# Differential attention's q and k kept in SBUF, and its scores taken as three 32-row products per map

## The chip, the cores and the metric

The kernel is one program on one core of a Trainium2 chip. The metric is the device time of one execution in microseconds (us); lower is better. The cores' engines are named as the profile names them: PE (TensorE matmul), PEld (its weight loads), DVE (VectorE), ACT (ScalarE), POOL (GpSimd), SP (SyncE, which here only issues DMAs).

## What is computed

Two layers of a block on 1024 tokens of width 1024. Each layer normalises x, projects it by `w_in` (1024 x 2472), and feeds three mixers whose outputs are joined and projected by `w_out`; then a squared-ReLU MLP of width 4096 follows. The three mixers are differential attention, latent attention (MLA) and a state space part with a short convolution. Only the first matters here, cut from the reference:

```python
DA_HEADS = 4; DA_QK = 32; DA_V = 64
q = q.reshape(b, s, DA_HEADS, 2, DA_QK)      # two maps per head
k = k.reshape(b, s, DA_HEADS, 2, DA_QK)
s1 = einsum('bqhd,bkhd->bhqk', q1b, k1) * DA_QK ** -0.5
s2 = einsum('bqhd,bkhd->bhqk', q2b, k2) * DA_QK ** -0.5
p = masked_softmax(s1, mask) - lam * masked_softmax(s2, mask)
o = einsum('bhqk,bkhe->bqhe', p, v)          # mask: chunks of 64 keys up to the query's own chunk
```

## The kernel before

Every large product is made from operands split in two float32r parts, `hi` and `lo`. The helper `mm3` (lines 189 to 193) issues hi·hi, hi·lo and lo·hi one after another into the same PSUM bank; these are lines L191, L192 and L193 of the profile. Split operands live in one SBUF tile, `split`, that is cut into numbered slots (`slot`, line 142); float32 scratch lives in `arena_f`. PSUM is two double banks (`bank_s`, `bank2`, line 139) and four single ones (`bank_t`, `bank_a`, `bank_b`).

One layer's mixer (line 1175) is written as Python generators that are woven together by shares: the in-projection `in_proj` (line 569), differential attention `attention` over four `da_head` generators (line 763), the state space part, MLA, and the loads of `w_out`. The program order that results is then reordered on each engine by the tile framework's scheduler, so that the order on PE is not that of the source; within an engine the instructions run in the order that the scheduler left.

`in_proj` walks through `w_in` by chunks of columns, with a chunk's weights loaded, and split by ACT (line 545) and by DVE or POOL (line 546), one chunk ahead. The first chunk holds q and k of the heads 0 and 1 ("pair 0", 128 feature rows each: two heads of two maps of 32 rows), then come v, MLA's low-rank columns (128x424 products), the six convolution chunks, with q and k of pair 1 between them, and z. Beside it, in layer 0 alone, a background stream (`mod_chunk`, line 408) loads 512 KB pieces of `w_ada` (line 415, on SP), multiplies them on POOL (L434), sums them on DVE (L436) and ends with tiny products on PE (L441, L443).

q and k of a pair leave PSUM feature-major in `qk` (line 595): ACT writes the hi part (L600), DVE the lo part (L601), into a ring of two half slots. Then POOL issues two DMAs per piece (L605) that write it to the DRAM tensor `d_qk` twice, so that the four blocks of 32 rows hold hi, hi, lo, lo for q and hi, lo, hi, lo for k. `da_head` (line 763) reads them back, for each map one DMA on POOL (L770) of 1024 KB, into a ring of three slots with all 128 rows filled. Thereby one product with 128 rows is the sum of all four of hi·hi, hi·lo, lo·hi and lo·lo:

```python
nc.tensor.matmul(S[:, c0:c1], Q[mp][:, tok], K[mp][:, c0:c1], start=True, stop=c1 < n)          # L786
nc.tensor.matmul(S[:, n - 64:n], self.chunk[:, 0:P], self.chunk[:, P:192], start=False, stop=True)  # L787
```

For each head, each of eight query tiles t and each of two maps this is one product per 512 keys out of n = 128 (t+1), and a mask product (L787) of 64 columns with a rank-one operand `chunk`. Then DVE takes the maximum (L723), ACT the exponential (L724), DVE joins the two maps (L794 to L797), PE transposes the probabilities (L749), ACT copies them (L752), PE multiplies them with v (L736), transposes the result (L759) and DVE scales it (L761). In the state space part, L1052 transposes rows that were read back from the DRAM tensor `d_xbc` (L1041), L1043 reads another part of it, L1063 uses that, and L1101 and L814 write results to `d_cc`. The first two heads run beside the in-projection's middle chunks, the last two beside z, the state space part and the start of MLA.

Of the kernel before, what the change touches and what calls it, by code (L numbers as in the profile page):

```python
# [11 lines left out]
F32R = mybir.dt.float32r  # L12
# [5 lines left out]
P = 128  # L18
T = 1024
NT = T // P  # L20
D = 1024
KD = D // P
# [22 lines left out]
class Arena:  # L45
    """Words of one tile, given out where they have been free for longest."""
# [12 lines left out]
    def _find(self, m, top):  # L59
        """Large pieces start at whole blocks; small ones keep to blocks already broken where they can."""  # L60
# [47 lines left out]
class Net:  # L108
    def __init__(self, ctx, tc, ins):
# [9 lines left out]
        # split operands: nine slots of 2048 words, then two blocks of a whole [KD, T]  # L119
# [11 lines left out]
    @contextmanager  # L131
    def phase(self, **banks):
        """The four single PSUM banks, by use."""
        with self.tc.tile_pool(name="psum", bufs=1, space=bass.MemoryType.PSUM, reuse_waits="tile") as self.psum:
            self.banks = banks
            yield
        self.psum = None
# [4 lines left out]
    def slot(self, i, *shape, off=0):  # L142
        """Words of the split operands from slot i on."""
# [8 lines left out]
    def ring(self, name, slots, *shape):  # L152
        """The next of the slots in turn."""
# [7 lines left out]
    def rsqrt(self, ssq, n, scale, eps):  # L161
        """1/sqrt(ssq*scale+eps) for [P, n] in plain arithmetic: a seed from the exponent, then Newton steps."""
# [15 lines left out]
    def rstd(self, ssq, y=None):  # L178
        """1/sqrt(ssq/D + eps) for [P, 1]: the table's root, then a Newton step."""
# [16 lines left out]
    def mlp(self, l, hT, y, bg, late, finish):  # L196
        """y = relu(h @ w_up)^2 @ w_down in groups of hidden tiles; finish(t) is called as each tile of y is complete."""
# [39 lines left out]
        for g, size in enumerate(GROUPS):  # L237
# [4 lines left out]
            if g == 0:  # L242
                # by halves of the tokens: the last tiles of h come later
# [37 lines left out]
    def setup(self):  # L281
# [5 lines left out]
        # rank-one products that mask the keys of a block's second chunk for the queries of its first  # L287
        m = F.get(192)
        nc.gpsimd.memset(m, 0.0)
        nc.gpsimd.memset(m[0:1, 0:64], -1.0e30)  # L290
        nc.gpsimd.memset(m[0:1, 128:192], 1.0)
# [7 lines left out]
        # silu(c), feature 8p+k at [p, k]  # L299
# [15 lines left out]
        self.d_qk = [dt(f"d_qk{l}", [4, 2 * P, 2, T], F32R) for l in range(DEPTH)]  # L315
# [5 lines left out]
    def rope_tables(self):  # L321
# [29 lines left out]
        # [cos | cos] and [-sin | sin]  # L351
# [56 lines left out]
    def mod_chunk(self, l, sec, q, W, lag=None):  # L408
        """W columns of section sec as a row of the DRAM table, in steps: the loads, the products, the sums.
        Without a lag the products run on the vector engine; with one Pool has them, and the sums follow so many steps  # L410
        later."""
# [43 lines left out]
    def mod_stream(self, todo, per, lag=None):  # L455
        """todo: arguments of mod_chunk; chunks run staggered, one started every so many steps."""
# [28 lines left out]
    def norm(self, x, a, b, xn, eng=None):  # L485
        """xn = (x*rstd)*a + b."""
# [25 lines left out]
    def finish(self, y, src, g, dst, t, x, u, junk):  # L512
        """x += rms(y)*g for one tile of tokens; y [P, D] in PSUM or SBUF; u and x hold [P, D], u may be y."""
# [10 lines left out]
    def stage_w(self, w, cols, step=None):  # L524
        """w[:, cols] for the column ranges given, as loads still to be split."""
# [12 lines left out]
    def load_w(self, stage, slot, eng=None):  # L538
        """hi/lo of staged columns as [P, 2, k, n] from a slot on."""
# [29 lines left out]
    def in_proj(self, l, hT, st, bg, late):  # L569
        """h @ w_in by chunks of columns, its weights one chunk ahead; yields after each PSUM bank or two.  # L570
        q, k of a pair of heads go to DRAM feature-major, v stays, the low-rank part goes to DRAM token-major,
        the convolved part feature-major; z is used at once by the state space part."""
# [5 lines left out]
        # the columns and the slot of each chunk  # L578
        chunks = [(pair(0), 2), (run(C_V), 0), (run(C_CQ, 212), 6), ([(C_CQ + 212, C_Z), (C_DT, C_DT + 8)], 2)]
        chunks += [(run(C_XBC, P), 5), (run(C_XBC + P), 6), (run(C_XBC + 3 * P), 2), (pair(1), 6), (run(C_XBC + 5 * P, P), 2)]  # L580
# [832 lines left out]
```

## Time and profile before

| what | value |
|---|---|
| runs, median (lowest to highest) | 2979.09 us (2963.41 to 2982.9), 3 runs |
| profiled execution | its time is known by its span alone, 2975.8 us: 3.3 us under the median of the runs |
| mean granted TensorE clock | 0.947 |
| PE, DVE, ACT, POOL busy | 90%, 52%, 32%, 21% of the span |
| DMA traffic | 273.19 MB, of it 33.58 MB on POOL's queue |
| `d_qk<-split` (L605) | 32 DMAs of 512 KB |
| `split<-d_qk` (L770) | 16 DMAs of 1024 KB |

In rows of the timeline the columns are: start in us, duration in us, engine, line, operation, output<-input, shapes, count, and in brackets how long the engine stood idle before it and what ended that. A matmul's duration is a latency; since matmuls are pipelined, what one costs is read from the distance between starts. In rows of the windows each engine's busy time is followed by its count of instructions, then come the granted clock, the share of DMA engines' time that was busy, and GB/s. In rows of the waits: total us, times, longest.

### The profile page before, as it was taken

What the parts mean: (1) busy time and instruction counts of PE and PEld (TensorE: products, weight loads), DVE (VectorE), ACT (ScalarE), POOL (GpSimd) and SP (SyncE); (2) the same over time, 40 slices, a digit from 0 to 9 for tenths busy, and PEclk for the clock granted to TensorE, in tenths of its full rate; (3) what the DMA queues carried; (4) which work ended last, traced back from release to release, by engine and by line L of the source; (5) the groups of instructions that cost most, each with busy time, mean ns of one, the idle gap of its engine ahead of it and who ended that gap; (6) DMA issues with size and microseconds to landing.
All of it is one profiled execution on the core that took longest, in us unless ns stands there. A gap on an engine that the chain in (4) does not pass through costs nothing. (4 is left out here: it accounts for less than half of the span.)

```text
span 2975.8 us, 33230 instructions
## 1 busy us (share of the span) xinstructions
PE 2683.2 (90%) x12402; PEld 2113.0 (71%) x12402; DVE 1554.6 (52%) x2861; ACT 941.5 (32%) x1827; POOL 623.3 (21%) x558
## 2 busy tenths in 40 slices
PE   5678779899899999999978895897998999999998
PEld 4556556676687877887757674665767888888887
DVE  7557457543835566666491563565446133433334
ACT  5233334544531112112242442344444221221222
POOL 1422224310311111111151122342003001111113
PEclk9889989899999999999989997898999999999999
DMA  6962632321423233233344245222123111111112
GB/s 215 197 113 85 154 74 77 113 70 43 164 78 100 79 99 104 74 107 91 99 139 108 64 125 104 66 86 92 56 99 113 43 50 50 57 43 44 57 43 99
DMA packets 275846, 273.19 MB, mean 92 GB/s; under 512 B 29730, under 2 KB 233700, under 8 KB 273636
## 3 DMA queue, kind: packets, MB, share of 16 engines
q1 hardware_dynamic: 258532, 237.47, 26.9%
q0 software_dynamic: 17152, 33.58, 5.3%
q8 instruction: 98, 1.61, 0.2%
q14 instruction: 64, 0.52, 0.1%
HBM read 221.34 MB, written 49.65 MB: 91 GB/s over the span
## 5 line engine op out<-in xcount | busy, mean ns | idle before, releaser
L191 PE MATMUL bank_b<-split 128*128 128x512 f32 (+2 forms) x1952 | 770.7, 395 | 30.0 <-ACT split L545 16.3
L192 PE MATMUL bank_b<-split 128*128 128x512 f32 (+2 forms) x1952 | 758.0, 388 | 9.5 <-DVE split L510 8.2
L193 PE MATMUL bank_b<-split 128*128 128x512 f32 (+2 forms) x1952 | 756.1, 388 | 1.2 <-DVE split L210 0.6
L191 PE MATMUL bank_s<-split 128*128 128x512 f32 (+2 forms) x1152 | 453.4, 396 | 8.8 <-ACT arena_f L724 3.9
L192 PE MATMUL bank_s<-split 128*128 128x512 f32 (+2 forms) x1152 | 449.9, 391 | 5.4 <-DVE split L1305 4.7
L191 PEld LDWEIGHTS bank_b<-split 128*128 128x128 f32 x1952 | 375.9, 193 | 110.7 <-ACT split L545 17.1
L193 PE MATMUL bank_s<-split 128*128 128x512 f32 (+2 forms) x1152 | 443.9, 389 | 0.5 <-DVE split L223 0.5
L192 PEld LDWEIGHTS bank_b<-split 128*128 128x128 f32 x1952 | 376.4, 193 | 77.4 <-DVE split L510 8.7
L193 PEld LDWEIGHTS bank_b<-split 128*128 128x128 f32 x1952 | 374.9, 192 | 73.2 <-issue 2.7
L274 DVE TENSOR_TENSOR arena_f<-arena_f,bank_s 128x1024 f32<-128x1024 f32 x208 | 253.2, 1219 | 313.4 <-PE bank_s L193 313.2
L222 POOL TENSOR_TENSOR arena_f<-arena_f 128x512 f32<-128x512 f32 x128 | 165.4, 1292 | 1004.2 <-ACT split L221 1000.1
L723 DVE TENSOR_REDUCE nm<-bank_s 128x1 f32<-128x128 f32 (+3 forms) x192 | 142.7, 752 | 238.0 <-PE bank_s L787 150.1
L191 PEld LDWEIGHTS bank_s<-split 128*128 128x128 f32 (+1 forms) x1152 | 217.8, 190 | 60.0 <-ACT arena_f L724 4.8
L192 PEld LDWEIGHTS bank_s<-split 128*128 128x128 f32 (+1 forms) x1152 | 218.6, 190 | 52.4 <-DVE split L1305 5.3
L193 PEld LDWEIGHTS bank_s<-split 128*128 128x128 f32 (+1 forms) x1152 | 218.1, 189 | 44.2 <-issue 0.9
L220 ACT ACTIVATE arena_f<-bank_b 128x512 f32<-128x512 f32 x128 | 76.1, 594 | 457.8 <-PE bank_b L193 457.6
L724 ACT ACTIVATE arena_f<-bank_s,nm 128x128 f32<-128x128 f32 (+3 forms) x192 | 141.9, 740 | 231.3 <-DVE nm L723 201.8
L231 ACT CAST split<-arena_f 128x1024 fp32r<-128x1024 f32 x64 | 67.4, 1052 | 391.9 <-PE bank_s L193 287.8
L223 DVE TENSOR_TENSOR split<-arena_f,split 128x512 fp32r<-128x512 f32 x128 | 91.3, 713 | 182.7 <-POOL arena_f L222 182.7
L430 DVE SCALAR_TENSOR_TENSOR arena_f<-arena_f,cond 128x128 f32<-128x128 f32 x448 | 153.0, 375 | 58.1 <-DMA arena_f<-in_w_ada 27.8
L736 PE MATMUL bank_a<-arena_f 128*64 128x256 f32 (+1 forms) x640 | 165.1, 385 | 12.8 <-ACT arena_f L752 8.6
L786 PE MATMUL bank_s<-split 128*128 128x512 f32 (+2 forms) x192 | 65.3, 405 | 96.7 <-DMA split<-d_qk 92.3
(259 smaller groups left out, 3078.8 us busy)
## 6 DMA issues: line engine op xcount, KB each, us to landing
arena_f<-in_w_ada SPq DMA_DIRECT2D x80, 512.0 KB
arena_f<-in_w_down SPq DMA_DIRECT2D x64, 512.0 KB
arena_f<-in_w_up SPq DMA_DIRECT2D x64, 512.0 KB
arena_f<-d_x SPq DMA_DIRECT2D x36, 512.0 KB
d_qk<-split POOLq DMA_DIRECT2D x32, 512.0 KB, 5.1
split<-d_qk POOLq DMA_DIRECT2D x16, 1024.0 KB, 25.9
d_x<-arena_f SPq DMA_DIRECT2D x24, 512.0 KB
arena_f<-in_w_in SPq DMA_DIRECT2D x20, 512.0 KB
```

The source lines that it names most:

```text
L191: mm(out, wh, xh, start=start, stop=False)
L192: mm(out, wh, xl, start=False, stop=False)
L193: mm(out, wl, xh, start=False, stop=stop)
L220: nc.scalar.activation(t, ps, AF.Relu)
L222: nc.gpsimd.tensor_mul(t, t, t)
L223: nc.vector.tensor_sub(r[:, 1, sl], t, f32(r[:, 0, sl]))
L231: nc.scalar.copy(wd[:, 0], st)
L274: nc.vector.tensor_add(y[t], y[t], ps)
L430: nc.vector.scalar_tensor_tensor(acc, in0=w[:, k], scalar=self.cond[:, k:k + 1], in1=acc, op0=ALU.mult, op1=ALU.add)
L723: nc.vector.tensor_reduce(nm, S[:, 0:n], axis=AX.X, op=ALU.max, negate=True)
L724: nc.scalar.activation(p[:, 0:n], S[:, 0:n], AF.Exp, bias=nm, accum_out=ls)
L736: nc.tensor.matmul(acc[:, 128:256] if half else acc, v[:, 2 * c + jj], e[:, 256:384] if half else e[:, jj * 256:jj * 256 + 256], start=c = ...
```

## The change

q and k no longer go through DRAM. `st["qk"]` gives each pair two whole slots (4 and 5 for pair 0, 0 and 1 for pair 1), and the eviction writes hi and lo straight into them; `d_qk`, its 32 writes and 16 reads and the rings are gone. A head's two maps then lie on the rows 0 to 31 and 32 to 63, or 64 to 95 and 96 to 127, of the same slots. Each map's scores are three products with 32 rows (hi·hi, hi·lo, lo·hi; lo·lo is no longer computed) where one with 128 rows was, written in the source with the two maps in turn, into two double banks that are taken together. The mask operand gets its nonzero row at 0, 32, 64 and 96, and the mask product uses the 32 rows of its map. The first convolution chunk's weights lie in slot 1, where they lay in slot 5. In the diff, comments that go are left out:

```diff
-        nc.gpsimd.memset(m[0:1, 0:64], -1.0e30)
-        nc.gpsimd.memset(m[0:1, 128:192], 1.0)
+        for b in range(0, P, 32):
+            nc.gpsimd.memset(m[b:b + 1, 0:64], -1.0e30)
+            nc.gpsimd.memset(m[b:b + 1, 128:192], 1.0)
...
-        self.d_qk = [dt(f"d_qk{l}", [4, 2 * P, 2, T], F32R) for l in range(DEPTH)]
...
+        st["qk"] = [[self.slot(n, 2, T) for n in q] for q in ((4, 5), (0, 1))]
...
-        chunks += [(run(C_XBC, P), 5), (run(C_XBC + P), 6), (run(C_XBC + 3 * P), 2), (pair(1), 6), (run(C_XBC + 5 * P, P), 2)]
+        chunks += [(run(C_XBC, P), 1), (run(C_XBC + P), 6), (run(C_XBC + 3 * P), 2), (pair(1), 6), (run(C_XBC + 5 * P, P), 2)]
...
-                e = self.ring("e", (5, 5.5), 2, 512)
+                e = st["qk"][m][i][:, :, hf * 512:hf * 512 + 512]
                 nc.scalar.activation(e[:, 0], ps, AF.Copy, scale=s)
                 nc.vector.scalar_tensor_tensor(e[:, 1], in0=ps, scalar=s, in1=f32(e[:, 0]), op0=ALU.mult, op1=ALU.subtract)
-                d = self.d_qk[l][:, m * P:m * P + P, i, hf * 512:hf * 512 + 512]
-                d = d.rearrange("(h a) r c -> r h a c" if i == 0 else "(a h) r c -> r h a c", a=2)
-                for a in range(2):
-                    nc.gpsimd.dma_start(d[:, :, a], e)
...
-        Q, K = [], []
-        for mp in range(2):
-            r = h * 64 + mp * 32
-            qk = self.ring("qk", (0, 1, 4), 2, T)
-            nc.gpsimd.dma_start(qk, self.d_qk[l][:, r:r + 32])
-            Q.append(qk[:, 0])
-            K.append(qk[:, 1])
+        Q, K = st["qk"][h // 2]
+        rows = [slice(r, r + 32) for r in (h % 2 * 64, h % 2 * 64 + 32)]
...
+                S = [self.bank2() for _ in range(2)]
+
+                for c0 in range(0, n, 512):
+                    c1 = min(n, c0 + 512)
+                    for a, b in ((0, 0), (0, 1), (1, 0)):
+                        for mp, rw in enumerate(rows):
+                            nc.tensor.matmul(S[mp][:, c0:c1], Q[rw, a, tok], K[rw, b, c0:c1], start=a == b, stop=a == 1 and c1 < n)
+                for mp, rw in enumerate(rows):
+                    nc.tensor.matmul(S[mp][:, n - 64:n], self.chunk[rw, 0:P], self.chunk[rw, P:192], start=False, stop=True)
                 for mp in range(2):
-                    S = self.bank2()
-                    for c0 in range(0, n, 512):
-                        c1 = min(n, c0 + 512)
-                        nc.tensor.matmul(S[:, c0:c1], Q[mp][:, tok], K[mp][:, c0:c1], start=True, stop=c1 < n)
-                    nc.tensor.matmul(S[:, n - 64:n], self.chunk[:, 0:P], self.chunk[:, P:192], start=False, stop=True)
                     p = F.get(n)
-                    self.softmax(S, n, p, self.sm(1, "nm"), ll[:, mp:mp + 1])
+                    self.softmax(S[mp], n, p, self.sm(1, "nm"), ll[:, mp:mp + 1])
```

In the changed program the two score lines are L781 (the products) and L783 (the mask), and the helpers' lines up to L546 keep their numbers. The scheduler makes another order of it. First, PE at layer 0's first scores. In the rows, the number behind `bank_s` or `bank_b` is the buffer, and "x3" counts equal rows. Before, the first products of both maps stood behind the first 128x424 products, which come after all of v's:

```order
L192 MATMUL bank_b_1058<-split_66 128x424
L193 MATMUL bank_b_1058<-split_66 128x424
L441 MATMUL bank_b_1095<-arena_f_67,ones_83 1x128
L443 MATMUL bank_b_1095<-arena_f_67,ones_83 1x128
L786 MATMUL bank_s_952<-split_66 128x128
L787 MATMUL bank_s_952<-chunk_mask_79 128x64
L786 MATMUL bank_s_1014<-split_66 128x128
L787 MATMUL bank_s_1014<-chunk_mask_79 128x64
L441 MATMUL bank_b_1134<-arena_f_67,ones_83 1x128
L443 MATMUL bank_b_1134<-arena_f_67,ones_83 1x128
L191 MATMUL bank_b_1149<-split_66 128x424
```

The same place of the changed program, at v's first products (128x256, L191 to L193):

```order
L328 MATMUL bank_b_614<-ident_68,arena_f_67 128x8
L191 MATMUL bank_b_682<-split_66 128x256
L191 MATMUL bank_b_708<-split_66 128x256
L781 MATMUL bank_s_946<-split_66 128x128 x3
L783 MATMUL bank_s_946<-chunk_mask_85 128x64
L192 MATMUL bank_b_682<-split_66 128x256
L193 MATMUL bank_b_682<-split_66 128x256
```

The first map's three products have moved up to v's first products, and they stand alone: the second map's (bank_s_947) come 26 rows later. Second, PE at the fourth and the later query tiles of head 0 in the changed program. The fourth tile's two maps stand in turn, as the source has them:

```order
L443 MATMUL bank_b_877<-arena_f_67,ones_89 1x128
L781 MATMUL bank_s_1129<-split_66 128x512
L781 MATMUL bank_s_1130<-split_66 128x512
L781 MATMUL bank_s_1129<-split_66 128x512
L781 MATMUL bank_s_1130<-split_66 128x512
L781 MATMUL bank_s_1129<-split_66 128x512
L781 MATMUL bank_s_1130<-split_66 128x512
L783 MATMUL bank_s_1129<-chunk_mask_85 128x64
L783 MATMUL bank_s_1130<-chunk_mask_85 128x64
L747 MATMUL bank_t_1110<-ident_68,arena_f_67 128x128 x2
```

The seventh tile's second map and the eighth tile's first map of the same head:

```order
L443 MATMUL bank_b_1373<-arena_f_67,ones_89 1x128
L781 MATMUL bank_s_1380<-split_66 128x512 x3
L781 MATMUL bank_s_1380<-split_66 128x384 x3
L783 MATMUL bank_s_1380<-chunk_mask_85 128x64
L747 MATMUL bank_t_1449<-ident_68,arena_f_67 128x128 x3
L781 MATMUL bank_s_1480<-split_66 128x512 x6
L783 MATMUL bank_s_1480<-chunk_mask_85 128x64
L441 MATMUL bank_b_1402<-arena_f_67,ones_89 1x128
```

Here each map's products stand by themselves, and other work lies between the two maps. Over the whole order 47 pairs of 512 columns out of 144 stand back to back on different rows (and 16 pairs each of 128, 256, 384 and of two masks); the score products, 576 in place of 192, with 128 mask products as before, form 102 runs, where there were 111. The order's matmuls change the shape of array that they use (32, 64 or 128 rows, 32, 64 or 128 columns, by their operands) 723 times, where they did 580 times.

## The prediction

> **What bounds the kernel now.** I read the page's busy table first, then the waits of PE, then the timeline of each engine around the longest of them, and the windows there. The first fence has lines of the page and one of the waits.
>
> ```profile
> span 2975.8 us, 33230 instructions
> PE 2683.2 (90%) x12402; PEld 2113.0 (71%) x12402; DVE 1554.6 (52%) x2861; ACT 941.5 (32%) x1827; POOL 623.3 (21%) x558
> L786 PE MATMUL bank_s<-split 128*128 128x512 f32 (+2 forms) x192 | 65.3, 405 | 96.7 <-DMA split<-d_qk 92.3
> ...
> PE bank_s L786 <- DMA split<-d_qk: 92.3, 6, 29.6
> ```
>
> PE is busy for 90% of the span and sets the time. Its largest single cause of standing still is the trip of q and k through DRAM: 92.3 us in six waits, the longest of PE's list. The timeline of PE shows where they lie; two shorter than 12 us are left out.
>
> ```profile
> 161.10 0.47 PE L786 MATMUL bank_s<-split 128*128 128x128 f32 x1 [22.96 <-DMA split<-d_qk]
> ...
> 226.96 0.48 PE L786 MATMUL bank_s<-split 128*128 128x128 f32 x1 [5.41 <-DMA split<-d_qk]
> ...
> 376.12 0.47 PE L786 MATMUL bank_s<-split 128*128 128x128 f32 x1 [20.79 <-DMA split<-d_qk]
> ...
> 1828.20 0.47 PE L786 MATMUL bank_s<-split 128*128 128x128 f32 x1 [29.63 <-DMA split<-d_qk]
> ```
>
> All are first products of a head, at n = 128. The windows tell why they last so long.
>
> ```profile
> 1760.00:1800.00 40.00, 36.97 (x166) 28.18 (x164) 18.23 (x34) 14.40 (x22) 16.24 (x16) 0.99 0.71 204
> ...
> 140.00:161.00 21.00, 0.00 (x0) 0.00 (x0) 0.00 (x0) 0.21 (x1) 0.00 (x0) 0.50 1.02 112
> ...
> split<-d_qk POOLq DMA_DIRECT2D x16, 1024.0 KB, 25.9
> ```
>
> While the reads of `d_qk` are under way the DMA engines are busy throughout (share 1.02) and move 112 GB/s; elsewhere 0.71 of their time moves 204. One read of 1 MB takes 25.9 us to land. So these reads also hold up what travels beside them. The next fence pairs a load that waits with the PE wait that follows: `w_ada` pieces at 228, `d_xbc` at 440, `w_in` at 1690, `d_cc` at 1889.
>
> ```profile
> 228.04 1.90 POOL L434 TENSOR_TENSOR arena_f<-arena_f,cond 128x1024 f32<-128x1024 f32 x1 [15.82 <-DMA arena_f<-in_w_ada]
> ...
> 233.94 0.90 PE L749 MATMUL bank_t<-ident,arena_f 128*128 128x128 f32 x3 [6.34 <-DVE arena_f L797]
> ...
> 439.98 1.09 PE L1052 MATMUL bank_t<-ident,arena_f 128*128 128x128 f32 x4 [9.88 <-DMA arena_f<-d_xbc]
> ...
> 1667.44 0.67 POOL L770 DMA_DIRECT2D split<-d_qk  x1 [4.30 <-PE bank_t L749]
> ...
> 1689.71 1.04 ACT L545 CAST split<-arena_f 128x1024 fp32r<-128x1024 f32 x1 [15.92 <-DMA arena_f<-in_w_in]
> ...
> 1690.81 0.79 PE L191 MATMUL bank_b<-split 128*128 128x512 f32 x1 [11.05 <-ACT split L545]
> ...
> 1889.49 0.48 ACT L752 COPY arena_f<-bank_t 128x384 f32<-128x384 f32 x1 [11.69 <-DMA d_cc<-arena_f]
> 1890.02 1.12 PE L1052 MATMUL bank_t<-ident,arena_f 128*128 128x128 f32 x4 [6.72 <-ACT arena_f L752]
> ```
>
> At 228.04 the `w_ada` piece lands 1.1 us after the q and k of 226.96; POOL's late product delays DVE, and L797 behind it. In the other three places a `d_qk` read was under way too (one issue is shown, at 1667.44, 22 us before the weights of 1689.71 land).
>
> **What it removes.** (1) The six waits: 92.3 us. (2) The waits of other loads: 6.34 + 9.88 + 11.05 + 6.72 = 34.0 us. (3) After each of these stalls the clock is at half for a while. Windows of PE from the end of a stall to the end of the low clock, eight of them, first, last and sum:
>
> ```profile
> 161.10:170.90 9.80, 8.03 (x25) 0.50 0.72 149
> ...
> 1890.00:1904.90 14.90, 14.18 (x49) 0.50 0.02 4
> sum 68.10, PE 58.51; mean PE 7.31
> ```
>
> 58.5 us of PE work at half speed cost 29 us more than at full speed. Shorter waits stay and will still drop the clock at times, so I take 20 of them and keep 29 for the range. (4) 48 DMA issues leave POOL's queue; POOL is busy for 21% and I give nothing for it. The eviction itself (ACT L600, DVE L601) is as long as before, only into other slots.
>
> **What it adds on PE.** The prices, from the distance of starts:
>
> ```profile
> 171.86 0.28 PE L786 MATMUL bank_s<-split 128*128 128x256 f32 x1
> 171.98 0.19 PE L787 MATMUL bank_s<-chunk_mask 128*128 128x64 f32 x1
> 172.01 0.36 PE L786 MATMUL bank_s<-split 128*128 128x256 f32 x1
> 172.21 0.20 PE L787 MATMUL bank_s<-chunk_mask 128*128 128x64 f32 x1
> 172.24 0.44 PE L191 MATMUL bank_b<-split 128*128 128x424 f32 x1
> 172.51 0.35 PE L192 MATMUL bank_b<-split 128*128 128x424 f32 x1
> ...
> 188.52 0.35 PE L193 MATMUL bank_b<-split 128*128 128x424 f32 x1
> 188.71 0.36 PE L191 MATMUL bank_b<-split 128*128 128x424 f32 x1
> 189.00 0.33 PE L759 MATMUL bank_a<-ident,arena_f 64*128 64x64 f32 x2
> 189.26 0.46 PE L192 MATMUL bank_b<-split 128*128 128x424 f32 x1
> 189.56 0.35 PE L193 MATMUL bank_b<-split 128*128 128x424 f32 x1
> ...
> 241.05 0.39 PE L191 MATMUL bank_b<-split 128*128 128x512 f32 x1
> 241.28 0.39 PE L192 MATMUL bank_b<-split 128*128 128x512 f32 x1
> ```
>
> 512 columns cost 0.23 us (241.28 - 241.05). 424 cost 0.19 (188.71 - 188.52). In the first block, two products of 256 and two masks hold PE from 171.86 to 172.24, and the next product is then 0.08 late (0.27 where 0.19 is usual): 0.46 for four, 0.115 each. That is the least that a matmul with weights of its own costs here, however few its columns; I use it up to 256, and 0.17 for 384 (estimate, 0.23 x 384/512).
>
> The score products go from 192 to 576, their sizes in the same proportion. Before: 96 of 512 (22.1), 64 of 128 and 256 (7.4), 32 of 384 (5.4), 128 masks (14.7): 49.6 us. After, if each costs what a 128-row product costs: 3 x 34.9 + 14.7 = 119.4. That adds 70 us. A product with 32 rows reads as many columns as one with 128, so it is no shorter; it could only run beside one on other rows. The order shown above decides how often that can be: 47 pairs of 512 stand back to back on different rows, and 16 of 384. If a pair took the time of one product, though not under its two weight loads (0.23), it would save 0.23 x 47 + (0.34 - 0.23) x 16 = 12.6 us. No row of this trace shows two row groups at once. Bounds: 57 and 70; I take the middle, 64.
>
> The change of array shape has a price too. At 189.00 two transposes of 64 rows stand between 128-row products: 0.10 before them (0.29 where 0.19 is usual), 0.11 behind them (0.30 for 0.19), and 0.26 for a pair that by its columns and loads needs about 0.11 (estimate, two at half of 0.115). 0.36 for two changes is 0.18 each. The order has 143 more changes: 26 us. Together 90 us on PE, which is the engine that sets the end.
>
> **What is late next.** The stalls end when something else becomes the last to arrive. At 161.10 the work behind L786 has its operands (the sums for L441 come from L436, first row below, done by 135), so PE goes on. In the second half of a mixer the chain convolution, write of `d_xbc`, read of `d_xbc` comes next:
>
> ```profile
> 132.94 1.99 DVE L436 TENSOR_REDUCE arena_f<-arena_f 128x128 f32<-128x1024 f32 x1
> ...
> 381.60 0.32 SPq L685 DMA_DIRECT2D d_xbc<-arena_f  x1
> ...
> 385.31 6.57 SPq L1043 DMA_DIRECT2D cz<-d_xbc  x6
> ...
> 390.10 0.67 PE L1063 MATMUL bank_b<-cz,arena_f 128*128 128x256 f32 x2
> ```
>
> It takes 8.5 us here behind head 2's wait, and head 2's scores, which can start at once now, stand ahead of it as cover. Without cover it costs 8.5 us in each layer, 17 in all; with it nothing. The double banks, taken for both maps together, can make PE wait for an exponential (L724) where the pairs stand in turn, and the projections' products queue behind it on PE. For both I put 15, between 0 and 40.
>
> **The sum.** -92.3 - 34 - 20 + 64 + 26 + 15 = -41. From the span 2975.8 that is 2935; the median of the runs lies 3.3 above the span, so I forecast 2938 us, 1.4% faster. A difference of about 1% can be told from none here.
>
> **The rivals.**
> *A. The products hide in what is left of the stalls* (faster than forecast). The sum over the four windows of the stages with scores (125 to 590 and 1590 to 2030 us):
>
> ```profile
> sum 905.00, PE 727.62 PEld 551.57 DVE 513.99 ACT 341.17 POOL 276.34; mean PE 181.91 PEld 137.89 DVE 128.50 ACT 85.29 POOL 69.09
> ```
>
> PE stands idle for 177 us there, 126 of which are (1) and (2). Products placed in the other 51, waits for DVE and ACT above all, cost nothing. If two thirds of these took 34 us of the new work, and nothing new came late, 2938 - 34 - 15 = 2889. For it: those waits are spread over all heads. Against: the order is set, and PE takes what stands next.
>
> *B. Weights are not preloaded in a 32-row shape* (slower than before). In the 128-row products a fresh operand is loaded behind the running product, or 512 columns couldn't repeat every 0.23 us. If products that follow each other on the same 32 rows had to wait for the load, each of the 480 products of 256 columns and more would cost 0.115 more, the 96 of 128 half that, the masks 0.03: 65 us, and 6 for the pairs: 2938 + 71 = 3009. It decides from 0.09 us per product on, where the gain of 41 is gone. Against it: the two L759 at 189.00 share their 64 rows and still take 0.26 in all. The Trainium skill, "TensorE: Matmul & The Clock Gate", Part 3 on packing small matmuls, says that a weight load overlaps running matmuls only when its row group differs. The trace disagrees for the full array, as the 0.23 us show; no run here shows it yet for 32 rows.
>
> *C. The loads are slow by themselves* (slower than before). Then the pieces of `w_ada` and `w_in` land as late without the `d_qk` reads beside them, (2) and half of (3) stay and half of (1) turns into waits for them: 46 + 34 + 10 = 90 less gained, 3028. For it: POOL waited 15.82 us for a piece of `w_ada`. Against: that piece lands together with q and k, and 204 GB/s are reached elsewhere.
>
> *D. It doesn't do what it says.* The words speak of two row groups side by side; the order has taken most of the pairs apart. That is in the sum already, and the gain doesn't hang on it. The same Part 3 reports four such products, one in each row group, at 3.07 times the speed of one after another; no run here shows it yet. An estimate by that page for two groups, nearly half the time, gives the lower bound above for the 47 pairs, and nothing for the other products.
>
> **Chances.** Forecast with its own range 2915 to 2965: 0.58. A: 0.20. B: 0.13. C: 0.09. Faster by over 1% needs under 2949: most of the forecast's case (0.44 of 0.58) and A, 0.64. Slower by over 1% (over 3009): about half of B and most of C, 0.13. Within 1%: 0.23. The range goes from A at 2889, less a little for waits before 125 us that the missing writes may shorten, to the middle between the forecast's end and C: 2885 to 2995.
>
> **What will show it.** No DMA stands in front of a score product; the long waits of L434, L545 and L1049 (L1052 before) on loads are gone, and PE's idle time falls by 100 us or more. In a run of three L781 of 512 columns the starts lie 0.23 apart; 0.34 would be B. Two on different rows side by side would show starts under 0.05 apart. A run of score products between 128-row products shows 0.1 late at each end. The MLP (620 to 1500 us) keeps its length. If waits for `w_ada` or `w_in` appear where q and k were, the prediction is wrong by C; if PE's busy time grows by 130 us or more, by B.

## The result, and the profile after

The changed kernel takes 2880.98 us (median of four runs, 2874.4 to 2889.2) against 2978.36 for the kernel before on the same chip: a ratio of 0.9684, 95% interval [0.9652, 0.9716]. It is 97 us faster where 41 were forecast, and lies 4 us below the range. The profiled execution took 2878.71 us.

The page of the changed kernel, the lines that answer to those of before:

```profile
span 2876.8 us, 33874 instructions
PE 2725.0 (95%) x12786; PEld 2136.1 (74%) x12786; DVE 1560.9 (54%) x2861; ACT 942.0 (33%) x1827; POOL 593.6 (21%) x516
```

The list of PE's waits in the changed kernel (us in all, times, longest):

```profile
PE bank_b L1281 <- DVE arena_f L1276: 18.1, 5, 9.3
PE bank_t L507 <- DVE split L510: 10.5, 2, 9.4
PE bank_t L865 <- DVE arena_f L861: 8.5, 1, 8.5
PE bank_b L192 <- DVE split L510: 8.0, 1, 8.0
PE bank_s L781 <- ACT arena_f L722: 7.8, 6, 4.0
...
PE bank_s L191 <- ACT arena_f L722: 4.8, 4, 1.8
...
PE bank_b L1258 <- DMA arena_f<-in_norm_g: 3.2, 1, 3.2
```

Two numbers tell the story. PE's idle time (span less busy) fell from 292.6 to 151.8 us: 141 gained. PE's busy time rose from 2683.2 to 2725.0: 42 spent. The difference, 99, is the change of the span. No DMA stands in front of a score product any more, and the only load among PE's waits is one of 3.2 us.

Where the scores' products cost their time, the timeline of PE shows two things that no row of before could show. First a query tile of 512 keys whose two maps stand in turn in the program, then three products of 512 and three of 256 columns on the same 32 rows:

```profile
1635.93 0.40 PE L191 MATMUL bank_b<-split 128*128 128x512 f32 x1
1636.26 0.97 PE L781 MATMUL bank_s<-split 32*128 32x512 f32 x6
1637.06 0.20 PE L783 MATMUL bank_s<-chunk_mask 32*128 32x64 f32 x2
1637.19 0.50 PE L192 MATMUL bank_b<-split 128*128 128x512 f32 x1
...
1656.64 0.40 PE L193 MATMUL bank_b<-split 128*128 128x512 f32 x1
1656.97 1.31 PE L781 MATMUL bank_s<-split 32*128 32x512 f32 x6
1658.12 0.19 PE L783 MATMUL bank_s<-chunk_mask 32*128 32x64 f32 x1
1658.24 0.50 PE L191 MATMUL bank_b<-split 128*128 128x512 f32 x1
```

Six products of 512 columns on two row groups pass in 0.80 us (1637.06 - 1636.26): three times 0.23 and 0.1 at the start, so each pair takes the time of one product, weight loads included. On one row group, three of 512 and three of 256 take 1.15: 3 x 0.23 + 3 x 0.115 and 0.1 at the start; the weights are preloaded there as on the whole array. Both runs begin 0.33 us behind the 128-row product ahead of them, where 0.23 is usual: 0.1 for the change of shape, and with the 0.1 at the start of the run 0.2 for entering it. On leaving, the next product comes 0.12 to 0.13 behind a mask, nearly on time. The Trainium skill, "TensorEngine Tiling (Array Packing)", Key Properties, says that different tiles can load weights and multiply in parallel; the 0.80 agrees.

### The profile page after: what moved, and what is told of

Same layout as the page of the kernel before. It is cut to its first block, busy times and chain, and to the rows that moved or that the text cites. A ratio compares the mean times of both kernels' runs of the same rounds, so it can differ in the third digit from the quotient of the medians.

```text
span 2876.8 us, 33874 instructions
## 1 busy us (share of the span) xinstructions
PE 2725.0 (95%) x12786; PEld 2136.1 (74%) x12786; DVE 1560.9 (54%) x2861; ACT 942.0 (33%) x1827; POOL 593.6 (21%) x516
## 4 chain that ended last, share of the span: by engine, by line
PE 73%; DVE 5%; DMA 2%; ACT 2%; issue 1%; POOL 1%; POOLq 0%; SPq 0%; DVEq 0%; ACTq 0%
PE bank_b L191 12%; PE bank_b L192 12%; PE bank_b L193 12%; PE bank_s L191 8%; PE bank_s L192 8%; PE bank_s L193 8%; PE bank_a L734 3%; PE bank_t L747 2%; PE bank_s L781 1%; PE bank_s L499 1%; PE bank_b L875 1%; DMA arena_f<-in_w_out 1%; PE bank_b L1074 1%; DVE rstd_t L185 1%; PE bank_t L441 1%
## 5 line engine op out<-in xcount | busy, mean ns | idle before, releaser
L191 PE MATMUL bank_b<-split 128*128 128x512 f32 (+2 forms) x1952 | 771.7, 396 | 11.4 <-DVE arena_f L614 4.6
L193 PE MATMUL bank_b<-split 128*128 128x512 f32 (+2 forms) x1952 | 754.7, 387 | 0.1
L191 PE MATMUL bank_s<-split 128*128 128x512 f32 (+2 forms) x1152 | 452.8, 396 | 8.5 <-ACT arena_f L722 4.8
L192 PE MATMUL bank_s<-split 128*128 128x512 f32 (+2 forms) x1152 | 449.6, 390 | 5.0 <-DVE split L1302 4.6
L193 PE MATMUL bank_s<-split 128*128 128x512 f32 (+2 forms) x1152 | 443.7, 388 | 0.0
L191 PEld LDWEIGHTS bank_b<-split 128*128 128x128 f32 x1952 | 375.5, 193 | 91.4 <-issue 7.0
L193 PEld LDWEIGHTS bank_b<-split 128*128 128x128 f32 x1952 | 374.5, 192 | 71.4 <-issue 2.4
L191 PEld LDWEIGHTS bank_s<-split 128*128 128x128 f32 (+1 forms) x1152 | 217.7, 189 | 59.0 <-ACT arena_f L722 5.6
L193 PEld LDWEIGHTS bank_s<-split 128*128 128x128 f32 (+1 forms) x1152 | 218.0, 189 | 43.4 <-issue 0.9
L220 ACT ACTIVATE arena_f<-bank_b 128x512 f32<-128x512 f32 x128 | 76.1, 595 | 473.8 <-PE bank_b L193 473.8
L722 ACT ACTIVATE arena_f<-bank_s,nm 128x384 f32<-128x384 f32 (+4 forms) x192 | 141.6, 739 | 181.5 <-DVE nm L721 158.7
L734 PEld LDWEIGHTS bank_a<-arena_f 128*64 128x64 f32 x640 | 76.5, 138 | 78.9 <-issue 27.3
```

What stands on the lines that cost most here:

```text
L191: mm(out, wh, xh, start=start, stop=False)
L192: mm(out, wh, xl, start=False, stop=False)
L193: mm(out, wl, xh, start=False, stop=stop)
L220: nc.scalar.activation(t, ps, AF.Relu)
L722: nc.scalar.activation(p[:, 0:n], S[:, 0:n], AF.Exp, bias=nm, accum_out=ls)
L734: nc.tensor.matmul(acc[:, 128:256] if half else acc, v[:, 2 * c + jj], e[:, 256:384] if half else e[:, jj * 256:jj * 256 + 256], start=c = ...
```

## The experiments

All times are medians in us. The last column is PE's busy time lost to a low clock, worked out from windows of 2.5 us as the sum of busy time x (1 - granted clock). PE's columns and the clock are those of the one profiled execution; in experiments 5 and 6 that was the slowest of the four (2919.4 and 2914.7 us). Experiments 3, 7, 8 and 9 are edits of experiment 1, 12 is one of the kernel before, the others are edits of the changed kernel.

| kernel | time | ratio to before, 95% | PE busy | PE idle | clock | lost to clock |
|---|---|---|---|---|---|---|
| before | 2978 | 1 | 2683.2 | 292.6 | 0.947 | 83 |
| changed | 2881.0 | 0.9684 [0.9652, 0.9716] | 2725.0 | 151.8 | 0.967 | 69 |
| 1 maps in turn | 2883.1 | 0.9687 [0.9656, 0.9717] | 2699.7 | 182.0 | 0.969 | 58 |
| 2 maps apart | 2901.4 | 0.9741 [0.9716, 0.9766] | 2748.0 | 150.0 | 0.964 | 76 |
| 3 one product | 2847.7 | 0.9560 [0.9539, 0.9581] | 2681.2 | 164.9 | 0.963 | 79 |
| 4 traffic | 2887.7 | 0.9705 [0.9673, 0.9737] | 2735.3 | 148.9 | 0.964 | 77 |
| 5 traffic, 2 KB | 2911.0 | 0.9777 [0.9740, 0.9813] | 2753.0 | 164.7 | 0.955 | 102 |
| 6 trip put back | 2902.2 | 0.9755 [0.9719, 0.9790] | 2741.9 | 171.0 | 0.959 | 90 |
| 7 zeros, 128 rows | 2946.4 | 0.9883 [0.9842, 0.9924] | 2780.9 | 163.4 | 0.957 | 101 |
| 8 zeros, 32 rows | 2898.9 | 0.9736 [0.9702, 0.9770] | 2724.9 | 171.4 | 0.963 | 74 |
| 9 in turn, ScalarE | 2880.4 | 0.9671 [0.9623, 0.9718] | 2711.4 | 169.9 | 0.966 | 69 |
| 10 changed, ScalarE | 2876.4 | 0.9664 [0.9610, 0.9718] | 2719.3 | 153.3 | 0.969 | 64 |
| 11 trip, all bytes | 2925.5 | 0.9822 [0.9777, 0.9866] | 2734.9 | 187.7 | 0.960 | 85 |
| 12 before, early read | 2980.6 | 1.0018 [0.9991, 1.0044] | 2677.7 | 298.2 | 0.946 | 78 |
| 13 same rows | 2912.5 | 0.9800 [0.9752, 0.9848] | 2765.5 | 145.7 | 0.963 | 81 |
| 14 all rows | 2869.0 | 0.9648 [0.9611, 0.9686] | 2702.3 | 162.7 | 0.979 | 34 |
| 15 all rows, ScalarE | 2876.1 | 0.9671 [0.9644, 0.9697] | 2707.6 | 166.3 | 0.977 | 39 |
| 16 all rows, GpSimd | 2873.5 | 0.9659 [0.9635, 0.9683] | 2708.8 | 163.4 | 0.977 | 39 |

### The order of the two maps (1, 2, 9, 10)

```
 for c0 ...: for a, b in ((0, 0), (0, 1), (1, 0)):
     for mp, rw in enumerate(rows):
-        nc.tensor.matmul(S[mp][:, c0:c1], Q[rw, a, tok], ...)
+        last = self.chained(S[mp][:, c0:c1], Q[rw, a, tok], ..., last, ...)   # issued behind last
```

Experiment 2 has the loop over `mp` outermost, around products and mask.

> The changed kernel with the score products of a query tile kept in the order of the source (map 0, map 1, map 0, map 1, ...), so that nearly every product stands next to one on the other 32 rows (597 neighbours on different rows, 4 on the same; in the changed kernel 244 and 367). Theory 1, products on different rows run wholly side by side, weight loads included: a pair takes the time of one product, 144 x 0.23 + 48 x 0.17 + 48 x 0.115 + 48 x 0.11 + 64 masks x 0.11 = 59 us where the changed kernel needs 108; about 45 us less, 2836 us, between 2830 and 2860 (up to 25 given back where map 0 now waits for map 1's bank). Rival A, the added products lie in PE's idle time: 2881, within 10. Rival 'one at a time' (a product needs the array for itself, the 97 us came from elsewhere): 2881, within 10.

> The changed kernel with the products of a query tile kept in the order of the maps: all of map 0, then all of map 1. Theory 1: only the last product of map 0 and the first of map 1 can still share the array; products and masks take up to 118 us instead of 108: 2885 to 2895, that is 45 to 60 us more than with the maps in turn. Rival 'one at a time': the same as with the maps in turn, within 5 us. Rival A: 2881, within 10, both.

In turn, PE is busy 25 us less than in the changed kernel, but stands idle 30 more, and nothing is gained: theory 1's time is missed, and the time is the one that both rivals gave, though PE's work did shrink. With the maps apart it takes 20 more (the intervals just touch). Theory 1 foresaw 45 to 60 between the two; it is 18: 48 of busy time (18 of it clock), less 32 of idle time. PE's waits of experiment 1 show who took some of it back. The first row stands in the changed kernel with 18.1 as well; the second stood there with 0.9:

```profile
PE bank_b L1289 <- DVE arena_f L1284: 19.5, 5, 10.6
PE bank_a L734 <- DVE arena_f L759: 13.7, 6, 4.6
```

The scaling of p times v waits in VectorE's queue, and the next p times v for the bank that it frees: 13 of the 30 us. The rest is spread over smaller waits. Experiments 9 and 10 move that scaling:

```
-        nc.vector.tensor_mul(out, po..., bcast(rl, 64))
+        for t in range(2):
+            nc.scalar.activation(out[:, t], po[:, t * 64:t * 64 + 64], AF.Copy, scale=rl[:, t:t + 1])
```

> The maps in turn, and the scaling of p times v that freed bank a (a product of VectorE) done by two instructions of ScalarE. In the first experiment PE was busy 25 us less than in the changed kernel and stood idle 30 us more, 14 of them in front of L734 for VectorE's L759. If VectorE's queue is what took the gain back: those waits go and 10 to 25 us are gained, 2856 to 2873. If it is the waits of the two maps for each other's bank, or whatever comes next to last: 2883, within 6.

> The changed kernel with only the move from VectorE to ScalarE. Here L734 waited 0.9 us for L759: 2881, within 6, by either theory; a gain like that of the run with the maps in turn would say that the move alone pays.

The wait of 13.7 goes, and the time stays within 3 us of experiment 1: other waits and 11 us of clock take its place. Neither differs from the changed kernel by what can be told.

Experiment 2 shows something else. There the program issues all of map 0 (A A A and its mask) ahead of all of map 1. Yet at 512 keys its timeline of PE shows

```profile
1644.72 0.49 PE L764 MATMUL bank_s<-split 32*128 32x512 f32 x1
1644.73 0.95 PE L766 MATMUL bank_s<-split 32*128 32x512 f32 x5
1645.52 0.19 PE L766 MATMUL bank_s<-chunk_mask 32*128 32x64 f32 x2
```

L764 is the first product of a tile, map 0's. Another starts 0.01 later; map 0's second can't, so it is map 1's, which has passed three waiting instructions. The six take 0.80 again. So products that wait for their own rows don't hold up those for other rows, and neighbours in the program are not the only pairs. (Of products on the same 32 rows, in experiment 13 below, only one pair starts within 0.04 us.) In runs of seven and seven, where map 0's first three products have 512 columns, map 1's first starts only with map 0's fourth (1651.58 in one), so the passing has a limit; where it lies was not tested.

### What a product, a pair and a change of shape cost (3, 7, 8, 13, 14)

```
3:  - for a, b in ((0, 0), (0, 1), (1, 0)):        + for a, b in ((0, 0),):
7:  + last = self.chained(S[0][:, c0:c0 + 64], self.chunk[:, 0:P], self.chunk[:, 64:P], last, ...)
8:  + last = self.chained(S[0][:, c0:c0 + 64], self.chunk[rows[0], 0:P], self.chunk[rows[0], 64:P], last, ...)
13: - rows = [..., h % 2 * 64 + 32)]                + rows = [..., h % 2 * 64)]
14: - rows = [slice(r, r + 32) for r in ...]        + rows = [slice(0, P)] * 2
```

> The maps in turn, and only hi x hi of the three products is computed: the output lacks the two corrections. Against the kernel with the maps in turn and three products this takes two thirds of the products away. Theory 1: 2/3 of 52 us = 35 us less, about 2801. Rival 'one at a time': 2/3 of 104 = 70 us less than that kernel. Rival A (hidden in idle time): less than 12 us.

35 us less than experiment 1, the difference that theory 1 had; its 2801 itself was missed by 47, as experiment 1's time had been. The products cost time, so they are not hidden. That the size fits is in part luck: PE's busy time fell by 18.5 only, with 21 us more of it lost to the clock, and 17 came out of idle time.

> The maps in turn, as in the first experiment (2883), with one product of 64 columns of zeros on all 128 rows behind the first pair of every run of up to 512 columns: 96 products and 200 changes of the array's shape more. The prediction's price of a change, 0.18 us: 36 + 11 for the products = 47 us more than 2883. By the starts in the changed kernel (a first 32-row product 0.09 late, a 128-row product behind a mask on time or 0.06 late): 0.06 a change, 12 + 11 = 23 more. Rival A (hidden in idle time): under 10 more.

> The same with the 64 columns of zeros on map 0's 32 rows: 96 products more, and no changes of shape to speak of (764 against 743). Theory 1, side by side: map 1's products pass meanwhile, so each costs 0 to 0.11: 0 to 11 us more than 2883. One at a time: 11 more. The difference from the run with 128 rows is the price of some 190 changes: 34 us by the prediction's 0.18, 12 by 0.06.

More than any theory gave: 63 and 16 over experiment 1, 47.5 apart. The table says why: 27 of the 47.5 are clock (101 against 74). Without it PE is busy 29 us more for 183 changes and 96 products that can't be shared, 0.10 to 0.16 a change. The timeline shows one of them:

```profile
1644.68 0.34 PE L766 MATMUL bank_s<-split 32*128 32x384 f32 x2
1644.96 0.30 PE L766 MATMUL bank_s<-chunk_mask 128*128 128x64 f32 x1
1645.18 0.61 PE L766 MATMUL bank_s<-split 32*128 32x384 f32 x4
1645.63 0.19 PE L766 MATMUL bank_s<-chunk_mask 32*128 32x64 f32 x2
```

A pair of 384, 0.17 when pairs follow each other, takes 0.28 ahead of the 128-row product, and that takes 0.22 where 0.115 would do: 0.1 each way. The two pairs behind it take 0.45 where 0.34 would do: the first is 0.1 late again.

> The changed kernel, in the same order of instructions, with both maps of a head computed from map 0's 32 rows (so map 1's scores are map 0's again): no two products can share the array. The prediction gave the sharing 6 us of its 64: 2887. If products on other rows pass waiting ones, as the run with the maps apart suggests (a program's A A A A B B B B ran as four pairs there), 164 pairs in the changed kernel start within 0.04 us of each other, not the 111 that are neighbours; at 0.11 to 0.23 each that is 18 to 38 us: 2900 to 2918.

Here no pair can share, and the order of instructions is the same. It takes 31.5 us more than the changed kernel: PE is busy 40.5 more, 12 of them clock, so sharing saves 28 us of PE's work. The forecast had 6.

> The same products and masks on all 128 rows (the scores are then sums over both heads and maps of the pair): no sharing and 149 changes of shape less than in the changed kernel. Against the run on the same 32 rows: 27 us less by the prediction's 0.18 per change, 10 to 16 by the 0.06 to 0.11 that starts in the changed kernel and the zero products suggest; none if shape costs nothing.

43.5 us less than on the same 32 rows, and 12 less than the changed kernel. Of PE's 63 us less, 47 are clock (34 lost against 81) and 16 are 149 changes of shape: 0.11 each. The distances of starts agree: from the last projection's product of 512 columns ahead of a run of scores to the run's second product it is 0.66 us in the changed kernel and 0.45 in experiment 14 (medians of 12 places), from the mask at its end to the second product of 512 columns behind it 0.46 and 0.43: 0.24 for the two changes of a run, nearly all of it on entering. The clock is what nobody had expected:

```profile
core 0: 2911.2 us, clock 0.963
```

```profile
core 0: 2865.0 us, clock 0.979
```

(span and granted clock, experiment 13 and then 14).

### A kernel on all rows (15, 16)

```
+ qz.append(self.slot(h // 2 * 4, 2, P, off=(2 * t + mp) % 8 * 256))
+ nc.gpsimd.tensor_scalar(qz[mp], f32(Q[:, :, tok]), only[map's 32 rows], None, op0=ALU.mult)
- nc.tensor.matmul(S[mp][:, c0:c1], Q[rw, a, tok], K[rw, b, c0:c1], ...)
+ nc.tensor.matmul(S[mp][:, c0:c1], qz[mp][:, a], K[:, b, c0:c1], ...)
```

> A whole kernel after the run on all rows: ScalarE copies the 128 columns of q of a map into a place of its own with the other 96 rows multiplied by 0 (128 copies of 128x256, some 0.4 us each), and the products run on all 128 rows. If the array's shape and the clock are what the 32-row form pays for: 2869 as in the run on all rows, up to 15 more where scores wait for a copy, so 2865 to 2884 and a clock of 0.975 or more. If the run on all rows was fast only because its values were others (rows of the other head in the sums): a clock of 0.967 and 2881 or more.

> The same with the copies on GpSimd, which is busy for 21% (128 copies of some 0.6 us): 2865 to 2884 by the first theory; 2890 or more where the copies stand behind the convolution's and the weights' work in its queue.

Same sums as in the changed kernel, no sharing, no added change of shape: clock 0.977 in both, as the first theory had it, and 5 and 7 us less than the changed kernel by the medians. (A copy took 0.50 us on ScalarE and 1.0 on GpSimd, more than was expected of either.) The intervals overlap, so they are not told apart from it. They do show that the values of experiment 14 were not the reason, and that the 28 us of sharing are given back by shape and clock.

### Was it the trip? (4, 5, 6, 11, 12)

```
4, 5: + the writes of d_qk as before;  + nc.gpsimd.dma_start(self.d_junk[l]..., self.d_qk[l][:, r:r + 32]...)
6:    + the writes of d_qk as before;  + nc.gpsimd.dma_start(x[rw], d[:, :, 0])   # into q and k in place
11:   6, and 512 KB per map to d_junk ahead of it
12:   - self.ring("qk", (0, 1, 4), 2, T)   + self.ring("qk", (4, 0, 1), 2, T)   # in the kernel before
```

> The changed kernel, plus the old writes of q and k to DRAM (33.6 MB in all with the reads) and reads of the same size at the same places of POOL's queue, from DRAM into a DRAM tensor that nobody uses: nothing waits for them. If the reads of q and k held up the loads beside them (term 2 of the prediction): waits of L434, L545 and L1049 for loads come back, 34 us and some 10 of clock, 2915 to 2930. Rival, the loads were late only because PE and the queues behind the stalled scores were late (no harm by contention): 2881, within 10.

> As the traffic run before it, but each read goes in four parts, cut into pieces of 2 KB as they were in the kernel before (in the earlier traffic run the reads took 15.5 us each with larger pieces; 25.9 before). Nothing waits for the data; POOL issues 48 DMAs more. If the reads of q and k held up the loads beside them: 2915 to 2930, with waits of PE, ACT or POOL for loads of 20 us or more. Rival, late only because what stood ahead of them was late: 2888, within 10.

In large pieces the same bytes cost 7 us, within the 10 of the rival. In pieces of 2 KB they cost 30, and in experiment 5's list of waits the one for `w_in` of the kernel before (16.3 us there) is back:

```profile
PE bank_b L191 <- ACT split L547: 14.6, 2, 9.9
```

Its list of DMA issues (KB each, us to landing) shows even the writes landing later, 9.3 us where the kernel before had 5.1:

```profile
d_qk<-split POOLq DMA_DIRECT2D x32, 512.0 KB, 9.3
```

33 us more of PE's busy time than in the changed kernel are lost to the clock. So such traffic can hold up `w_in`, as term 2 has it, when it goes in small pieces; in PE's list nothing stands for `w_ada` or `d_xbc`. How much the reads of the kernel before did is only bounded by this: the expectation took its pieces for 2 KB, and they were not. The pages' lines on POOL's queue (packets, MB, share of 16 engines) are, for the kernel before, experiment 4 and experiment 5:

```profile
q0 software_dynamic: 17152, 33.58, 5.3%
```

```profile
q0 software_dynamic: 9984, 33.56, 3.7%
```

```profile
q0 software_dynamic: 42496, 33.66, 4.4%
```

By the sizes in the traces the reads went in 2048 packets of 8 KB before, in 256 of 64 KB in experiment 4 and in 8192 of 2 KB in experiment 5. The kernel before lies between the two, and so, if the cost goes with the pieces, does what its reads cost others: between 7 and 30 us.

> The changed kernel with the trip put back: q and k are written to DRAM as before and each map's 32 rows are read back into the places where they are, with half the bytes of the kernel before per read (512 KB), and the scores wait for that. Theory: the wait itself is what the change removed; PE waits again for q and k in front of a head's first score product, 40 to 90 us in all, and the clock falls behind it: 2925 to 2990. Rival C of the prediction (loads slow by themselves, PE would have waited anyway): under 10 us more than the changed kernel, 2891 at most.

> The trip put back as before, and ahead of each map's read 512 KB more are copied from DRAM to DRAM in pieces of 2 KB, so that POOL's queue carries 1 MB per map as in the kernel before. The trip with half of that cost 21 us, with 4 us of PE's waits in front of the score products. If the bytes made the waits of the kernel before: 30 to 60 us of such waits, 2935 to 2960. If it was the late issue (there the reads went out at 125.8, when slots came free; with the trip put back at 111): few waits again, 2905 to 2920.

Both theories miss. The trip put back costs 21 us, 44 with all the bytes, but in neither does a score product wait for q or k. In the profiled executions, 36 and 46 us longer than that of the changed kernel, PE stands idle 19 and 36 us more and loses 21 and 16 us more to the clock; in 11 there is a wait of 13.6 for `w_in` again.

The edit changed one thing more: the order that the scheduler made. Head 0's first score product starts at 82.2 us in the changed kernel and at 126.7 in experiment 6, 2.7 behind the landing of its reads (issued from 111.0 on, landed by 124.0), and PE has other work until then. So these runs don't show that the trip takes no time, only that it can be covered.

> The kernel before, with the three places for q and k taken in the order 4, 0, 1 instead of 0, 1, 4: place 4 is free at once, place 0 only when the values' weights have been used, so the first read can go out some 12 us earlier. Late issue: the wait of 23 us at 161 shrinks by 10 or more, and the kernel takes 2955 to 2970. Bytes: 2979, within 6, since the same 1 MB pieces share the DMA engines.

The reads went out at 119.1 instead of 125.8, 7 us earlier and not 12, and it changed nothing, as the timeline of PE and then the list of DMA issues show:

```profile
161.73 0.48 PE L786 MATMUL bank_s<-split 128*128 128x128 f32 x1 [29.70 <-DMA split<-d_qk]
```

```profile
split<-d_qk POOLq DMA_DIRECT2D x16, 1024.0 KB, 33.2
```

The reads took 33.2 us each where they took 25.9, and the scores began when they had begun before; PE's waits for them are 119.2 us in all, where they were 92.3. So the six waits of the kernel before came neither from these 7 us of delay nor from the bytes alone. Two things are left. One is the form of its reads: the first three, of 1 MB each into 128 rows, were issued from 125.8 us on and landed from 161.1 to 165.0, where the first eight of experiment 6, 256 KB each, were issued from 111.0 on and had landed by 127.6. The other is the place of the scores in PE's order: PE stood still for them from 138.1 on, 12 us after the first read's issue, and in experiment 6 came to them 16 us after it. At this place the landing is the larger part; neither was tried by itself, and it stays open.

## Why the forecast was 57 us too slow

*What it removes.* (1) held: 92.3 us, all six waits. (Not all are first products of a head: the one at 226.96 is that of a second map, whose read went out only at 206.7.) (2) was 10 too small, because only the longest wait of each group was counted: with the 9.9 for `d_xbc` the groups make 44.1. The groups of the kernel before were

```profile
PE bank_b L191 <- ACT split L545: 16.3, 4, 11.1
...
PE bank_t L749 <- DVE arena_f L797: 9.7, 5, 6.3
...
PE bank_t L1052 <- ACT arena_f L752: 8.2, 5, 6.7
...
PE bank_s L786 <- ACT arena_f L724: 4.4, 7, 1.2
PE bank_s L191 <- ACT arena_f L724: 3.9, 4, 1.7
```

in the list of its waits. None of the first three has a like among the waits after. (3) 14 of 20 came.

*The new waits* (15) hardly came. The waits for an exponential rose from 8.3 (last two rows) to 12.6; the chain through `d_xbc` shows no wait at all, so head 2's scores did cover it. In all, 141 of idle time against 111 forecast: 30 of the 57, of which these two steps explain 21; the rest is spread.

*The products and shapes* (64 + 26) are the step that failed most. PE's busy time rose by 42; with the 14 of clock that is 56 of work where 90 stood. Of the 34, 22 are sharing: 28 (experiment 13) for 6. The step was "the order shown above decides how often that can be", and with it the floor of two weight loads under a pair. A pair's loads run side by side too, small products share as well (in experiment 1 pairs of 256 follow each other every 0.12 us and pairs of 384 every 0.18, under the floor of 0.23), and products pass waiting ones on other rows: 130 pairs of score products start within 0.04 us in the changed kernel, where 95 stand as neighbours in its program, and one does in experiment 13. (Another 34 pairs have a mask in them and prove little: 27 such start together on the same rows too, in experiment 13.) Another 10 are the change of shape, 0.11 (experiment 14) instead of 0.18, on 143 changes. All these splits set PE's busy time and the clock of one execution of a kernel against those of another.

*The signals.* Idle time fell by more than 100; same-row products 0.23 apart; pairs within 0.01; 0.1 late on entering a run, and 0.1 again within it, but hardly on leaving it; the MLP of layer 0 as long as before (first to last L220: 679 us before, 678 after). One sign came in part only: POOL's L434 still waits 46.6 us for `w_ada`, 14.6 at the longest, where it waited 66.9; no wait of PE follows from it.

*The rivals.* A gives 2889, near the result, but the work did not hide: without sharing (experiment 13) PE is busy 40.5 us more and idle only 6 less. Something of A is true all the same: of the 48 us of busy time between experiments 1 and 2, 32 come back as idle time, so how much is hidden hangs on the order. B is refuted by the 1.15 us above, C by PE's waits after. D too: the two groups do run side by side, more often than the order promises. That this makes the change fast is not so. One at a time on all rows is as fast (experiments 14 to 16); the gain is the 141 us of idle time.

## What to carry to other kernels

Price concurrent row groups by a run that takes the sharing away and one that uses all rows: here 28 us of sharing were paid back by 16 of shape changes and by the clock. When a stall goes, add up whole groups of waits, not their longest members. And when work saved on PE doesn't shorten the span, look in the waits for the queue that has become the last, and expect another behind it: here 13 of 30 us stood in front of VectorE's queue, and taking them away (experiment 9) left the time as it was.

## What was not expected of the hardware

The clock goes with the shape of the products. In the three kernels with all score products on 128 rows after the change (14 to 16) PE loses 34 to 39 us to a low clock, in the thirteen that use 32 rows 58 to 102, some of them with less idle time. The granted clock says the same in every run: 0.974 to 0.979 in the 16 runs of those three, 0.955 to 0.971 in the runs of the thirteen. (The kernel before, on 128 rows too, loses 83, with 293 us of idle time.) Windows of the changed kernel show a spell at half clock with PE busy nearly throughout:

```profile
1850.00:1855.00 5.00, 5.00 (x24) 3.65 (x23) 3.40 (x14) 2.31 (x4) 0.00 (x0) 1.00 0.30 71
1855.00:1860.00 5.00, 4.40 (x14) 3.15 (x13) 3.77 (x7) 3.46 (x7) 2.38 (x1) 0.51 0.25 77
1860.00:1865.00 5.00, 5.00 (x17) 3.89 (x17) 3.84 (x5) 1.69 (x3) 0.00 (x0) 0.50 0.23 69
1865.00:1870.00 5.00, 5.00 (x20) 4.17 (x20) 2.47 (x6) 2.51 (x4) 1.99 (x2) 0.50 0.06 23
```

(the number behind POOL's is the granted clock). The largest wait in this stretch is 0.60 us, ahead of a run of score products. The Trainium skill, "TensorE: Matmul & The Clock Gate", Part 1, ties the clock to how busy PE has been; that a product on a quarter of the rows counts as less busy would fit these rows, but was only argued here; it does not account for experiment 3, which has a third of such products and loses 79 us where experiment 1 loses 58. Products on one row group pass waiting ones on another, as in experiment 2. The passing, and the microseconds lost to the clock, are from one execution of each kernel; the times of the table are medians of four to ten.
